# One step of a hybrid trunk layer: other buffers for cached values and sample states, other places in the engines' order

## The chip, the cores and the metric

The kernel runs on one core of a Trainium2 chip. A core has TensorE (PE: matmuls, with weight loads beside them), VectorE (DVE), ScalarE (ACT), GpSimd (POOL) and SyncE (SP, which issues transfers), each with an instruction stream of its own that runs in order, and 16 DMA engines. ACT and POOL issue transfers too. The metric is the device time of the core in microseconds, as the median of the runs; less is better.

## The reference, cut to what matters

A layer takes 1024 prompt tokens and 8 sample tokens (one new token each, with caches). The parts, in the order of the kernel:

```
p  = x @ w_in                       # 1024 -> 3592 columns: q, k, v of 8 attention heads; u (q, k, v), z, a, b of 4 delta heads
delta heads (prompt):  q, k, v = silu(causal conv(u));  q, k normalised
    chunks of tokens:  T = I + strict_lower(beta * k k^T * decay);  solve T [u | w] = [v beta | k beta e^g]
    state carried over the chunks;  o = q S;  RMS norm;  * silu(z)
delta heads (samples): S = S e^g;  mem = k S;  S = S + k ((v - mem) beta);  o = q S       # S from state_b_ssm
attention (prompt):    softmax over dilated windows (128,1) (512,4) (2048,16) with a relative bias, merged by denominators
attention (samples):   the same over cache_a_k, cache_a_v (512 rows) and the new row
h  = LayerNorm(alpha x + mix @ w_out)
y  = LayerNorm(alpha h + MoE(h))    # 4 groups x 8 experts, top 1 group, top 2 experts in it
```

Outputs: y of prompt and samples, the key and value windows, the new rows, the delta states and the convolution states. All is fp32.

## The kernel before

Products keep fp32 by a split: a number is held as a high part (a cast) and a low part (the difference), and a product is three matmuls, xh wh, xl wh, xh wl (L278 to L280, 128x344 each). `weight(c0)` loads 128 columns of w_in on SP's queue, casts the high part on ACT (`his`, L254) and subtracts the low part on DVE (`los`, L255).

The stages, by time:

- 0 to 40 us: x is loaded and transposed; the a and b columns are projected.
- 40 to 460: four delta heads. For each: features (convolution, squares for the norms with ACT L483), then the triangular solve inside 16-blocks on DVE, which is a substitution column by column (`column`, L521 to L525, then L530 to L532, columns again, and the spread of the result, L535), then the larger blocks by matmuls on PE (`inverse`), then the scan over chunks (L583 to L613) and the gate. The projections of the next columns stand between these steps in PE's order and fill its waits.
- In the same stretch, `delta_sample` (L667) does the samples' delta work: convolution on POOL, tanh on ACT (L685), products and norms; for each head it loads the 8 states (si, L673), multiplies them with k and q (pkq, 16 small matmuls, L720) and copies the result (skq, L721). A second time, after attention 0, it loads the states again, updates them on POOL (L759 to L761, with rows wb) and stores them (out_ssm_sample, L762).
- 460 to 770: attention of four pairs of heads. Each softmax step has a score matmul (L850, L851, with low key parts kl from DVE L823), a minimum on DVE (L852), exponentials on ACT (L857), transposes on PE (L866), copies pT (ACT L868, DVE L870) and the output matmul (L875). `scores_sample` loads cached keys kc and multiplies them by the query on POOL (L904), and DVE sums (L905). In the last pair w_out is loaded and split too (L1052, L1054 on ACT, L1055 on DVE).
- 750 to 950: mixing with w_out (`mixed`, L1124), the samples' attention over cached values (`attention_sample`: v loads by `cache_rows`, L773 to L779, on POOL's queue, products pav L937), the first layer norm, routing and the lists of the experts.
- 950 to 1530: 32 experts, their weights in pieces of 1 MB (`piece`, L956, on SP's queue), split on ACT and DVE (L1343, L1344).
- 1530 to 1580: the last layer norm.

Big tiles share named slots: a tile with the name of a slot waits until the last reader of the tile before it is done. The slots of 2048 columns are w (2), kq (2), dtf and xy; those of 1024 columns are U (2), acc, vt, ktl (2), vh (2), gb, ft, qk (2), zt (2), os and z2. The four cached-value tiles all lie in xy. The pieces of the first experts lie in these slots too: piece 2 and 3 in kq, 4 in dtf, 8 in xy. `PIECE_AT` says which of them are issued behind which `mixed(t)`; the others are issued before the first.

The order of each engine is fixed at compile time by a scheduler. `after(later, earlier)` (L260) adds an edge to it that has no semaphore: it only says that `later` comes behind `earlier` in the order. `SUMS` and `WOD` feed such edges: pair and softmax step behind which a sum of scores, or a w_out split, is placed.

Of the kernel before, what the change touches and what calls it, by code (L numbers as in the profile page):

```python
# [12 lines left out]
AF = mybir.ActivationFunctionType  # L13
OP = mybir.AluOpType
# [4 lines left out]
P = 128  # L19
S = 1024  # L20
NS = 8
# [3 lines left out]
NT = S // P  # L25
# [3 lines left out]
HB = 4  # L29
# [3 lines left out]
AHEAD = 2  # L33
FLY = 5
XGB, YB, WHB, AHB, EHB, ELB = 2, 1, 5, 1, 2, 2
SUMS = ((0, 8), (1, 8), (2, 4), (3, 4))
GROUPS = (4, 7, 8, 9)
RNK = ((0, 3), (4, 8), (7, 8))
PTD = 3
# [4 lines left out]
ADD = ((8, 7, 8),)  # L44
FAST = True
ATS = 3
PIECE_AT = {3: 8, 4: 6}
LATE = 29
LN_ORDER = (0, 1, 2, 3, 4, 5, 6, 7, 8)
LN_ACT = (1, 3, 5, 7, 8)  # L50
# [60 lines left out]

U_ = lambda j, h: 1536 + (4 * j + h) * P
DJ = 2
WOD = [(3, k + 1) for k in range(8)]
FIRST = (3, 6)
ABA = (1, 3)
EARLY_D = (0,)
# [5 lines left out]
def body(ctx, tc, I, O, C):  # L123
    nc = tc.nc
# [66 lines left out]
    def T8(tag, name):  # L191
        return s8.tile([P, 2048], F32, tag=tag, name=name, bufs=S8[tag])
# [22 lines left out]
    def T4(tag, name):  # L215
        n, b = W4[tag]
        turn[tag] = (turn.get(tag, -1) + 1) % b
        return four(f"{tag}{turn[tag]}", n, name)
# [24 lines left out]
    loads, his, los, decays = {}, {}, {}, {}  # L243
# [11 lines left out]
        los[c0] = nc.vector.tensor_tensor(out=lo, in0=rw, in1=hi.bitcast(F32), op=OP.subtract)  # L255
        return hi, lo

    values, parts, roots, exps, last, inverse, stores, sums, minima = {}, {}, {}, {}, {}, {}, {}, {}, {}

    def after(later, earlier):  # L260

        tc.add_manual_dep(later.ins, earlier.ins.name, mybir.DependencyInfo(mybir.DependencyClass.NoSync, mybir.DependencyReason.DATA),
                          reason="projections fill the wait for a chain")
# [38 lines left out]
    for t in range(NT + 1):  # L302
        n = P if t < NT else NS
# [4 lines left out]
        for b in range(2):  # L308
            ps = tps(f"xps{t}_{b}")
# [21 lines left out]
    for t in range(NT + 1):  # L331
        n = P if t < NT else NS
# [107 lines left out]
    def delta(h, kq):  # L440
# [34 lines left out]
        for b in range(2):  # L475
            for j, f in enumerate((q2, k2)):
                ps = tps(f"fps{h}_{b}_{j}")
                for n in range(4):
                    t = 4 * b + n
                    nc.tensor.transpose(ps[:, n, :], f[:, t * P:(t + 1) * P], ident)  # L480
                for n in range(4):
                    t = 4 * b + n
                    nc.scalar.activation(out=junk, in_=ps[:, n, :], func=AF.Square, accum_out=ss[:, j, t:t + 1])  # L483
                    if j == 1:
                        nc.vector.tensor_scalar(out=ktl[:, t, :], in0=ps[:, n, :], scalar1=etail[:, t, h:h + 1],
                                                scalar2=None, op0=OP.mult)
# [34 lines left out]
        def column(f, j0, k0, k):  # L521

            n = k - j0
            nc.vector.tensor_tensor(out=xm[:, :, :n], in0=f[:, :, :n, k - k0], in1=xb[:, :, k:k + 1].to_broadcast([P, NT, n]), op=OP.mult)
            nc.vector.tensor_tensor(out=xb[:, :, j0:k], in0=xb[:, :, j0:k], in1=xm[:, :, :n], op=OP.subtract)  # L525

        for k in range(15, 8, -1):
            column(fc, 8, 9, k)
        pr = dtf[:, S:S + 512].rearrange("p (t j k) -> p t j k", j=8, k=8)
        nc.vector.tensor_tensor(out=pr, in0=fa[:, :, :, 7:15], in1=xb[:, :, None, 8:16].to_broadcast([P, NT, 8, 8]), op=OP.mult)  # L530
        nc.vector.tensor_reduce(out=xm, in_=pr, axis=AX.X, op=OP.add)
        nc.vector.tensor_tensor(out=xb[:, :, 0:8], in0=xb[:, :, 0:8], in1=xm, op=OP.subtract)  # L532
        for k in range(7, 0, -1):
            column(fa, 0, 1, k)
        nc.vector.tensor_tensor(out=x.rearrange("p t (b j) -> p t b j", j=16), in0=xb[:, :, None, :].to_broadcast([P, NT, 8, 16]),  # L535
                                in1=m16.rearrange("p (b j) -> p b j", j=16)[:, None, :, :].to_broadcast([P, NT, 8, 16]), op=OP.mult)

        vt = yield
# [127 lines left out]
    def delta_sample():  # L666
        tps = lambda name: psd.tile([P, 4, P], F32, tag="c", name=name)  # L667
        state = I["state_b_ssm"][0].rearrange("s h d e -> d h s e")
        out = O["ssm_sample"][0].rearrange("s h d e -> d h s e")

        def state_in(h, again):
            t = T4(("ft", "z2")[h % 2] if again else "U", f"si{h}_{again}")[:, :S]
            nc.sync.dma_start(out=t.rearrange("p (s e) -> p s e", e=P), in_=state[:, h])  # L673
            return t

# [6 lines left out]
        for i in range(3):  # L682
            nc.gpsimd.tensor_tensor(out=tmp, in0=cst[:, :, i, :].rearrange("p s t -> p t s"), in1=wv(i), op=OP.mult)
            nc.gpsimd.tensor_tensor(out=acc, in0=acc, in1=tmp, op=OP.add)
        nc.scalar.activation(out=tmp, in_=acc, func=AF.Tanh, scale=0.5)  # L685
        f2 = sm_t("f2", [P, 12, NS])
        nc.vector.scalar_tensor_tensor(out=f2, in0=tmp, scalar=1.0, in1=acc, op0=OP.add, op1=OP.mult)
        q2, k2, v2 = f2[:, 0:4, :], f2[:, 4:8, :], f2[:, 8:12, :]
# [10 lines left out]
        nc.vector.reciprocal(out=pw[SH:2 * SH, 2:3], in_=pw[SH:2 * SH, 3:4])  # L699
        nc.gpsimd.tensor_tensor(out=pw[:SH, 2:3], in0=pw[:SH, 3:4], in1=nhalf[:SH, 0:1], op=OP.pow)  # L700
        roots["s"] = nc.gpsimd.tensor_tensor(out=pw[:2 * SH, 3:4], in0=pw[:2 * SH, 3:4], in1=half[:2 * SH, 0:1], op=OP.pow)
        dg = T4("os", "dg")[:3 * SH, :4 * SH]
        nc.vector.tensor_scalar(out=dg[:, :3 * SH], in0=ident[:3 * SH, :3 * SH], scalar1=pw[:3 * SH, 2:3], scalar2=None, op0=OP.mult)
        nc.vector.tensor_scalar(out=dg[:, 3 * SH:], in0=ident[:3 * SH, SH:2 * SH], scalar1=pw[:3 * SH, 3:4], scalar2=None, op0=OP.mult)
        ps = tps("spb").rearrange("p a b -> p (a b)")
# [10 lines left out]
        for h in range(HB):  # L716
            si = state_in(h, 0)
            pk = tps(f"pkq{h}").rearrange("p a b -> p (a b)")
            for s in range(NS):
                nc.tensor.matmul(pk[:, 2 * s:2 * s + 2], si[:, s * P:(s + 1) * P], f2[:, h:h + 5:4, s], start=True, stop=True)  # L720
            nc.vector.tensor_copy(out=skq[:, h], in_=pk[:, :2 * NS])  # L721

        w = sm_t("ws", [P, HB, NS])
        t1 = sm_t("t1s", [P, HB, NS])
# [9 lines left out]

        ps = tps("pwt").rearrange("p a b -> p (a b)")
        nc.tensor.transpose(ps[:SH, :P], fl(w), ident)
        wr = T4("os", "wr")[:SH, :P]
        nc.vector.tensor_copy(out=wr, in_=ps[:SH, :P])
        nc.gpsimd.dma_start(out=wr_d.rearrange("h (s e) -> (h s) e", e=P), in_=wr)
        yield  # L740
# [168 lines left out]
    def attention_sample(tps, avs):  # L909
# [15 lines left out]
        nc.vector.tensor_copy(out=p1, in_=ps[:, 0:64])  # L925
        nc.vector.tensor_copy(out=p2[:ROWS2], in_=ps[:ROWS2, 64:128])
        for pr in range(4):
            v12 = T8("xy", f"v_{pr}")
            v1, v2 = tiles(v12), tiles(v12[:, S:])
            cache_rows(v1, v2, vf, 2, pr)  # L930

            pav = tps(f"pav{pr}")
            for a in range(2):
                for n, (p_, v) in enumerate(((p1, v1), (p2, v2))):
                    r = P if n == 0 else ROWS2
                    for c in range(4):
                        nc.tensor.matmul(pav[32 * c:32 * c + 32, a, :], p_[:r, 4 * a:4 * a + 4, :].rearrange("p s h -> p (s h)"),  # L937
                                         v[:r, 4 * a + c, :], start=(n == 0), stop=(n == 1))
            av = avs[:, pr % 2 * 256:pr % 2 * 256 + 256].rearrange("p (a b) -> p a b", b=P)
            nc.scalar.copy(out=av, in_=pav[:, 0:2, :])  # L940
            pat = tps(f"pat{pr}")
            for a in range(2):
                nc.tensor.transpose(pat[:, a, :], av[:, a, :], ident)
            for j in range(2):
                r = slice(64 * j, 64 * j + 64)
                nc.vector.tensor_copy(out=mixS[r, HB + pr, :].rearrange("p (a c) -> p a c", c=4), in_=pat[r, 0:2, 2 * pr + j:2 * pr + j + 121:40])
# [122 lines left out]
        after(his[-k - 1], exps[p_][max(n - 1, 0)])  # L1069
    for h in VTD:  # L1070
        after(values[h], last[VTD[h]])
    after(roots[HB - 1], roots["s"])
    after(sums["s"], last[0, 0])
    for h in range(HB):
        if FILL[h] is not None:
# [5 lines left out]
    with ph12:  # L1081
# [214 lines left out]
            nc.vector.tensor_scalar(out=gat, in0=pl[:, NE:2 * NE], scalar1=1.0 / ALPHA, scalar2=None, op0=OP.mult)  # L1296

        for i in range(NA):
            if i not in PIECE_AT.values():
                piece(i, i)  # L1300
        for t in range(NT + 1):
            if t == ATS:
                attention_sample(tps, avs)
            if t != QS:
                mixed(t)
            else:
                mixed_samples()
            if t in PIECE_AT:
                piece(PIECE_AT[t], PIECE_AT[t])
            if t + 1 in GROUPS:  # L1310
                listed = route(max([g for g in (0,) + GROUPS if g <= t]), t + 1)
        for t, t0, i in ADD:
# [281 lines left out]
```

## Time and profile before

| what | us |
| --- | --- |
| median of 3 runs | 1577.39 |
| lowest and highest run | 1575.81, 1586.39 |
| the profiled execution | 1581.44 |
| its span, first to last instruction | 1579.7 |
| PE busy in the span | 1437.3 (91%) |
| DVE busy | 1105.5 (70%) |
| ACT busy | 879.8 (56%) |
| POOL busy | 352.4 (22%) |

The mean granted clock of TensorE is 0.94 of full speed. The rows further down come from this one execution; its times count from the first instruction. A row of a window gives its bounds, its length, the busy time (and count) of PE, of PE's weight loads, of DVE, ACT and POOL, then the granted clock as a share of full speed, the DMA share, and GB/s. In a row of instructions the bracket at the end gives the idle time of the engine just before and what ended it.

### The profile page before, as it was taken

How to read it: one execution, taken by the hardware profiler on the slowest of the kernel's cores; microseconds unless marked ns; L12 is line 12 of the kernel's file. 1: busy time of each engine (PE TensorE's matmuls, PEld its weight loads, DVE VectorE, ACT ScalarE, POOL GpSimd, SP SyncE). 2: the span in 40 equal slices, each digit the busy share in tenths (PEclk: the TensorE clock that was granted, in tenths of full speed). 3: DMA queues.
4: the chain of work that ended last, by engine and by line, in shares of the span. 5: the costliest groups of instructions: out<-in, count | busy, mean ns of one | idle time of the engine just before them, and what ended most of it. 6: DMA issues, size and time to landing. Idle time of an engine off the chain costs nothing. (4 is left out here: it accounts for less than half of the span.)

```text
span 1579.7 us, 22960 instructions
## 1 busy us (share of the span) xinstructions
PE 1437.3 (91%) x8084; PEld 1183.1 (75%) x8085; DVE 1105.5 (70%) x2105; ACT 879.8 (56%) x1754; POOL 352.4 (22%) x346
## 2 busy tenths in 40 slices
PE   5979999989999889997987988999999999999970
PEld 3969888888987768874764766888888888888860
DVE  4576686857444545355532767999999999999977
ACT  3323434432243334344320117999999999999974
POOL 7020222214022420102111112111221112211115
PEclk9989999999899989995998978999999999999995
DMA  5221110114133342325655276999999999999965
GB/s 175 101 90 41 43 41 17 53 36 113 25 110 100 128 101 67 98 97 195 180 184 129 96 280 249 359 361 373 362 355 352 361 367 365 362 353 364 341 193 215
DMA packets 140016, 309.39 MB, mean 196 GB/s; under 512 B 13483, under 2 KB 71775, under 8 KB 139888
## 3 DMA queue, kind: packets, MB, share of 16 engines
q1 hardware_dynamic: 113928, 259.21, 45.5%
q0 software_dynamic: 14720, 33.92, 8.6%
q10 hardware_dynamic: 11248, 14.75, 2.9%
q8 instruction: 65, 1.06, 0.3%
q14 instruction: 55, 0.45, 0.1%
HBM read 284.04 MB, written 45.24 MB: 208 GB/s over the span
## 5 line engine op out<-in xcount | busy, mean ns | idle before, releaser
L1344 DVE TENSOR_TENSOR wl<-p,wh 128x512 fp32r<-128x512 f32 x436 | 270.2, 685 | 1.4 <-ACT wh L1343 1.4
L1343 ACT CAST wh<-p 128x512 fp32r<-128x512 f32 x436 | 254.2, 633 | 18.8 <-PE h L1380 8.5
L278 PE MATMUL pp<-xh,w 128*128 128x344 f32 x672 | 231.8, 345 | 2.0 <-ACT w L254 1.5
L280 PE MATMUL pp<-xh,w 128*128 128x344 f32 x672 | 223.9, 333 | 9.0 <-DVE w L255 9.0
L279 PE MATMUL pp<-xl,w 128*128 128x344 f32 x672 | 224.9, 335 | 0.0
L1378 PE MATMUL h<-wh,eh 128*128 128x512 f32 x512 | 206.8, 404 | 0.0
L1379 PE MATMUL h<-wl,eh 128*128 128x512 f32 x512 | 205.6, 402 | 0.4 <-DVE wl L1344 0.4
L1380 PE MATMUL h<-wh,el 128*128 128x512 f32 x512 | 201.3, 393 | 0.0
L278 PEld LDWEIGHTS pp<-xh,w 128*128 128x128 f32 x672 | 130.6, 194 | 12.5 <-issue 6.4
L280 PEld LDWEIGHTS pp<-xh,w 128*128 128x128 f32 x672 | 130.8, 195 | 11.2 <-DVE w L255 9.3
L279 PEld LDWEIGHTS pp<-xl,w 128*128 128x128 f32 x672 | 130.8, 195 | 2.1 <-issue 1.5
L1350 POOL MEMSET xg<- 128x1024 f32 x32 | 30.5, 953 | 400.2 <-PE xp L1363 396.3
L1379 PEld LDWEIGHTS h<-wl,eh 128*128 128x128 f32 x512 | 96.7, 189 | 25.6 <-DVE wl L1344 7.9
L1344 DVE TENSOR_TENSOR wl_d<-p,wh_d 128x512 fp32r<-128x512 f32 x188 | 115.5, 684 | 0.0
L1343 ACT CAST wh_d<-p 128x512 fp32r<-128x512 f32 x188 | 109.5, 621 | 3.2
L1378 PEld LDWEIGHTS h<-wh,eh 128*128 128x128 f32 x512 | 96.9, 189 | 18.7 <-ACT eh L1365 0.2
L1380 PEld LDWEIGHTS h<-wh,el 128*128 128x128 f32 x512 | 96.5, 188 | 18.5 <-DVE el L1366 0.2
L1419 PE MATMUL py<-wh_d,al 128*128 128x512 f32 x248 | 96.9, 391 | 0.0
L1417 PE MATMUL py<-wh_d,ah 128*128 128x512 f32 x248 | 96.6, 389 | 0.0
L1418 PE MATMUL py<-wl_d,ah 128*128 128x512 f32 x248 | 96.5, 389 | 0.0
L1124 PE MATMUL op<-wo,qkm 128*128 128x512 f32 x256 | 89.7, 425 | 0.0
L857 ACT ACTIVATE sc<-sc,mx 128x128 f32<-128x128 f32 (+7 forms) x64 | 49.6, 776 | 70.7 <-DVE mx L852 63.8
(463 smaller groups left out, 2852.4 us busy)
## 6 DMA issues: line engine op xcount, KB each, us to landing
p<-in_w_up SPq DMA_DIRECT2D x58, 1024.0 KB
p<-in_w_gate SPq DMA_DIRECT2D x51, 1024.0 KB
p<-in_w_down SPq DMA_DIRECT2D x47, 1024.0 KB
rw<-in_w_in SPq DMA_DIRECT2D x28, 512.0 KB
p_vh<-in_w_down SPq DMA_DIRECT2D x12, 512.0 KB
p_ktl<-in_w_gate SPq DMA_DIRECT2D x10, 512.0 KB
p_ktl<-in_w_down SPq DMA_DIRECT2D x10, 512.0 KB
skew_d<-bias_d SPq DMA_DIRECT2D x1, 4608.0 KB
```

Of the source, the lines that this page charges most:

```text
L278: nc.tensor.matmul(ps, wh[:, k, :], xh[:, k, s], start=(k == 0), stop=False)
L279: nc.tensor.matmul(ps, wh[:, k, :], xl[:, k, s], start=False, stop=False)
L280: last[c0, g] = nc.tensor.matmul(ps, wl[:, k, :], xh[:, k, s], start=False, stop=(k == KD - 1))
L1124: mixes[t] = nc.tensor.matmul(pss[b], m[:, k, :], wo[k][:, w, cs[b]], start=(k + i == 0), stop=(k + i == KD + 1))
L1343: nc.scalar.copy(out=wh, in_=src)
L1344: nc.vector.tensor_tensor(out=wl, in0=src, in1=wh.bitcast(F32), op=OP.subtract)
L1378: nc.tensor.matmul(ps, eh[:, k, :], wh, start=(k == 0), stop=False)
L1379: nc.tensor.matmul(ps, eh[:, k, :], wl, start=False, stop=False)
L1380: nc.tensor.matmul(ps, el[:, k, :], wh, start=False, stop=(k == KD - 1))
L1417: nc.tensor.matmul(py[b], ah[:, k, :], wh, start=(k == 0), stop=False)
L1418: nc.tensor.matmul(py[b], ah[:, k, :], wl, start=False, stop=False)
L1419: nc.tensor.matmul(py[b], al[:, k, :], wh, start=False, stop=(k == 3))
```

## The change

The cached values of the four pairs get the slots dtf, kq, kq and xy. Since pieces 2, 3 and 4 use the same slots, they are now issued behind `mixed(3)`, with piece 8. The samples' states of the first pass come in halves of one kq tile and no longer in U; in the second pass in ft and os and no longer in ft and z2. Two small tiles that lay in os (dg, wr) get a tile of their own. The score sums of pairs 2 and 3 and the w_out splits move to later softmax steps. In the order, one edge goes and four come: the samples' tanh behind the last square of head 3 (ACT), the samples' state products of head 0 behind the inverse of head 3 (PE), their first copy behind the spread of head 3's substitution (DVE), and the first column of head 0's substitution behind the weight split of head 1's q columns (DVE).

```diff
-SUMS = ((0, 8), (1, 8), (2, 4), (3, 4))
+SUMS = ((0, 8), (1, 8), (2, 10), (3, 12))
...
-PIECE_AT = {3: 8, 4: 6}
+PIECE_AT = {3: (8, 4, 2, 3), 4: (6,)}
...
-WOD = [(3, k + 1) for k in range(8)]
+WOD = [(3, k + 4) for k in range(8)]
...
-                    nc.scalar.activation(out=junk, in_=ps[:, n, :], func=AF.Square, accum_out=ss[:, j, t:t + 1])
+                    squares[h] = nc.scalar.activation(out=junk, in_=ps[:, n, :], func=AF.Square, accum_out=ss[:, j, t:t + 1])
...
         for k in range(15, 8, -1):
-            column(fc, 8, 9, k)
+            i = column(fc, 8, 9, k)
+            substituted.setdefault(h, i)
...
+        si2 = T8("kq", "si2")
+
         def state_in(h, again):
-            t = T4(("ft", "z2")[h % 2] if again else "U", f"si{h}_{again}")[:, :S]
+            t = T4(("ft", "os")[h % 2], f"si{h}_{again}")[:, :S] if again else si2[:, h % 2 * S:h % 2 * S + S]
...
-        nc.scalar.activation(out=tmp, in_=acc, func=AF.Tanh, scale=0.5)
+        tanhs["s"] = nc.scalar.activation(out=tmp, in_=acc, func=AF.Tanh, scale=0.5)
...
-        dg = T4("os", "dg")[:3 * SH, :4 * SH]
+        dgw = sm_t("dgw", [P, P])
+        dg = dgw[:3 * SH, :4 * SH]
...
-                nc.tensor.matmul(pk[:, 2 * s:2 * s + 2], si[:, s * P:(s + 1) * P], f2[:, h:h + 5:4, s], start=True, stop=True)
-            nc.vector.tensor_copy(out=skq[:, h], in_=pk[:, :2 * NS])
+                i = nc.tensor.matmul(pk[:, 2 * s:2 * s + 2], si[:, s * P:(s + 1) * P], f2[:, h:h + 5:4, s], start=True, stop=True)
+                products.setdefault(h, i)
+            copies[h] = nc.vector.tensor_copy(out=skq[:, h], in_=pk[:, :2 * NS])
...
-        wr = T4("os", "wr")[:SH, :P]
+        wr = dgw[:SH, :P]
...
-            v12 = T8("xy", f"v_{pr}")
+            v12 = T8(("dtf", "kq", "kq", "xy")[pr], f"v_{pr}")
...
-    after(roots[HB - 1], roots["s"])
+    after(tanhs["s"], squares[HB - 1])
+    after(products[0], inverse[HB - 1])
+    after(copies[0], spread[HB - 1])
+    after(substituted[0], los[U_(0, 1)])
...
-            if t in PIECE_AT:
-                piece(PIECE_AT[t], PIECE_AT[t])
+            for i in PIECE_AT.get(t, ()):
+                piece(i, i)
```

## Rows read from the trace of the kernel before

**Rows 1.** Windows by stage (columns as told in the section on the profile).
```profile
0.00:960.00 960.00, 866.11 (x5415) 714.54 (x5417) 536.75 (x1173) 323.25 (x779) 216.32 (x241) 0.92 0.34 105
960.00:1530.00 570.00, 569.62 (x2665) 467.63 (x2664) 536.98 (x888) 539.04 (x950) 112.77 (x91) 1.00 0.97 351
1530.00:1579.70 49.70, 1.57 (x7) 0.96 (x6) 31.79 (x46) 17.48 (x26) 23.27 (x14) 0.56 0.53 185
```

**Rows 2.** PE's waits by releaser, whole span: total us, times, longest.
```profile
PE pav L937 <- DMA v<-in_cache_a_v: 13.5, 3, 5.3
PE pp L280 <- DVE w L255: 9.0, 1, 9.0
PE s L851 <- DVE kl L823: 6.7, 1, 6.7
...
PE o L875 <- DVE pT L870: 6.2, 3, 5.3
...
PE ks L587 <- DVE st L602: 4.4, 3, 4.0
```

**Rows 3.** Waits of SP's queue, 900 to 1530 us.
```profile
SPq L956 <- DVE wl L1344: 99.1, 50, 14.8
```

**Rows 4.** Windows behind the longest waits.
```profile
112.70:116.00 3.30, 3.25 (x11) 3.25 (x12) 0.00 (x0) 0.00 (x0) 0.14 (x1) 0.51 0.58 158
377.10:414.60 37.50, 34.27 (x186) 32.96 (x185) 15.79 (x51) 3.56 (x7) 7.00 (x8) 0.77 0.37 82
557.40:567.50 10.10, 10.10 (x32) 7.20 (x32) 3.58 (x12) 2.47 (x10) 0.56 (x1) 0.55 0.92 209
713.00:754.00 41.00, 31.80 (x101) 18.83 (x101) 23.26 (x44) 17.57 (x35) 7.68 (x5) 0.50 0.53 182
827.00:868.00 41.00, 27.49 (x190) 19.18 (x188) 8.07 (x14) 3.39 (x7) 5.87 (x9) 0.83 0.57 130
```

**Rows 5.** Timeline of DVE, 99 to 117 us: start, duration, engine, line, operation.
```profile
100.54 1.35 DVE L524 TENSOR_TENSOR xm<-xy,xb 128x56 f32<-128x56 f32 x1 [2.27 <-ACT xy L512]
...
111.48 1.22 DVE L255 TENSOR_TENSOR w<-rw,w 128x1024 fp32r<-128x1024 f32 x1
```

**Rows 6.** Timelines of ACT, and of PE, around the same wait.
```profile
101.16 1.04 ACT L254 CAST w<-rw 128x1024 fp32r<-128x1024 f32 x1
...
112.75 0.65 PE L280 MATMUL pp<-xh,w 128*128 128x344 f32 x1 [9.03 <-DVE w L255]
```

**Rows 7.** Timeline of DVE, 347 to 352 us.
```profile
349.76 0.26 DVE L687 SCALAR_TENSOR_TENSOR f<-tmps 128x96 f32<-128x96 f32 x1 [4.13 <-ACT tmps L685]
```

**Rows 8.** Timeline of PE, 384 to 402 us.
```profile
393.21 0.32 PE L278 MATMUL pp<-xh,w 128*128 128x344 f32 x1
393.37 1.84 PE L720 MATMUL pkq<-f,si 128*128 128x2 f32 x16
```

**Rows 9.** Window of head 3's substitution, matmuls of L278 alone.
```profile
377.10:414.60 37.50, 14.92 (x39) 8.79 (x39) 0.77 0.37 82
```

**Rows 10.** Timeline of DVE, 526 to 590 us.
```profile
529.80 4.71 DVE L821 TENSOR_TENSOR qs<-qT,qs 64x512 fp32r<-64x512 f32 x2 [0.19 <-ACT qs L819]
...
556.64 0.68 DVE L823 TENSOR_TENSOR kl<-kT,ksa 64x512 fp32r<-64x512 f32 x1 [10.44 <-DMA out_ssm_sample<-si]
...
583.88 1.22 DVE L905 TENSOR_REDUCE sc<-kc 128x16 f32<-128x1024 f32 x1
```

**Rows 11.** Timeline of POOL, 545 to 575 us.
```profile
553.47 0.97 POOL L777 DMA_DIRECT2D kc<-in_cache_a_k  x1 [0.30 <-POOL si L761]
...
566.94 4.71 POOL L904 TENSOR_TENSOR kc<-kc,qb 128x1024 f32<-128x1024 f32 x2 [10.62 <-DMA qb<-qkv_d]
```

**Rows 12.** Timeline of DVE, 712 to 737 us.
```profile
723.13 1.22 DVE L905 TENSOR_REDUCE sc<-kc 128x16 f32<-128x1024 f32 x1 [4.22 <-POOL kc L904]
...
727.53 0.55 DVE L870 COPY pT<-pps 128x384 f32<-128x384 f32 x1
```

**Rows 13.** Timeline of POOL, 700 to 880 us.
```profile
839.12 0.92 POOL L777 DMA_DIRECT2D v<-in_cache_a_v  x1 [12.14 <-PE pav L937]
```

More of the change, by code (lines that the diff above doesn't have):

```diff
@@ L256, in weight @@
         return hi, lo
-    values, parts, roots, exps, last, inverse, stores, sums, minima = {}, {}, {}, {}, {}, {}, {}, {}, {}
+    values, parts, roots, exps, last, inverse, stores, sums, minima, substituted, spread, squares, tanhs, products, copies = ({} for _ in range(15))
     def after(later, earlier):
@@ L523, in column @@
             n = k - j0
-            nc.vector.tensor_tensor(out=xm[:, :, :n], in0=f[:, :, :n, k - k0], in1=xb[:, :, k:k + 1].to_broadcast([P, NT, n]), op=OP.mult)
+            i = nc.vector.tensor_tensor(out=xm[:, :, :n], in0=f[:, :, :n, k - k0], in1=xb[:, :, k:k + 1].to_broadcast([P, NT, n]), op=OP.mult)
             nc.vector.tensor_tensor(out=xb[:, :, j0:k], in0=xb[:, :, j0:k], in1=xm[:, :, :n], op=OP.subtract)
+            return i
         for k in range(15, 8, -1):
-            column(fc, 8, 9, k)
+            i = column(fc, 8, 9, k)
+            substituted.setdefault(h, i)
         pr = dtf[:, S:S + 512].rearrange("p (t j k) -> p t j k", j=8, k=8)
@@ L534, in delta @@
             column(fa, 0, 1, k)
-        nc.vector.tensor_tensor(out=x.rearrange("p t (b j) -> p t b j", j=16), in0=xb[:, :, None, :].to_broadcast([P, NT, 8, 16]),
+        spread[h] = nc.vector.tensor_tensor(out=x.rearrange("p t (b j) -> p t b j", j=16), in0=xb[:, :, None, :].to_broadcast([P, NT, 8, 16]),
                                 in1=m16.rearrange("p (b j) -> p b j", j=16)[:, None, :, :].to_broadcast([P, NT, 8, 16]), op=OP.mult)
@@ L1298, in body @@
         for i in range(NA):
-            if i not in PIECE_AT.values():
+            if not any(i in at for at in PIECE_AT.values()):
                 piece(i, i)
```

## The prediction

> **What bounds the kernel.** I read the busy shares by stage first. Up to 960 us TensorE (PE) is busy 866 of 960 us at a granted clock of 0.92; from 960 to 1530, the experts, it is busy 569.6 of 570 at 1.00; behind that lies a tail of 50 us with almost no matmuls [rows 1]. So the experts run at PE's limit, and what starts them earlier ends the kernel earlier, one for one, if their weights keep up. They do: the weight queue stood 99 us in that stage waiting for buffers to come free, not for bytes [rows 3]. The question is then which of the 94 idle microseconds ahead of 960, and which of the slow-clock ones, the change takes away. PE's waits by releaser name them: 13.5 us on cached values, 9.0 on one weight split, 6.7 on attention's low keys, 5.3 on a transposed-probability copy, 4.0 on a state update [rows 2]. Last I read windows just behind these waits: the granted clock is 0.51 to 0.55 there, that is at the lower of its two levels (1.2 of 2.4 GHz), for 3.3 us after the wait that ends at 112.7 and 10 us after the one that ends at 557.4 [rows 4]. A removed wait therefore gives back its length and about half of the slow stretch behind it.
>
> **A, weight split before the substitution.** The first column of head 0's substitution starts on VectorE (DVE) at 100.54 and the low half of the next weight, L255, comes only at 111.48, behind the whole chain [rows 5]. Its cast on ScalarE (ACT) was done at 101.16 + 1.04 = 102.20 [rows 6]. The new edge puts L255 first: 102.2 + 1.22 = 103.4, and PE ran dry at 112.75 - 9.03 = 103.72 [rows 6]. The wait goes: 9.0. Behind it 3.25 us of matmuls at 0.51 become 1.6: another 1.6. The substitution ends some 2 us later; projections cover it, since PE has weights again. A = 10.6.
>
> **B, samples' delta work behind head 3.** Today ACT and DVE wait in order for the samples' tanh and product (DVE 4.13 us at L687 [rows 7]), and head 3's scan stands behind them: 4.0 on PE [rows 2]. The edge behind the last square takes that wait off: 4.0. From 377.1 to 414.6 PE then runs head 3's fill at a mean clock of 0.77, busy 34.3 us [rows 4], because sixteen-matmul groups on state tiles (pkq) and DVE copies are woven into the substitution. At full clock a projection matmul starts every 0.16 us and a pkq group takes 1.84 [rows 8]. The stretch holds 39 x 3 = 117 projection matmuls [rows 9] = 18.7 us, four pkq groups = 7.4, and 0.5 for the rest: 26.6 in place of 37.5, a gain of 10.9. The groups still run, behind inverse[3]. B = 14.9. What may come back: the states now go through two halves of one buffer, so heads 2 and 3 load only after heads 0 and 1 were read. Below, nothing (projections cover it); above, two waits like the longest one for cached values, 2 x 5.3 = 10.6 [rows 2]. I take 4, as projections are left to run.
>
> **C, second state load.** DVE stood 10.44 us at L823 until a state's output transfer had freed a slot [rows 10], and PE 6.7 behind it [rows 2]. With the states in ft and os, and no longer in z2, that slot is free: 6.7. The 10.1 us behind at 0.55 [rows 4] would take 5.6: 4.5 more. C = 11.2. What is late next: the os half waits for earlier outputs, so POOL's state products end later, and the cached keys of pair 1 are loaded right behind them, at 553.47 [rows 11]. The product of these keys starts at 566.94, its first half ends near 569.3, and the sum that reads it, on DVE in front of softmax steps, came at 583.88 [rows 10, 11]: 14.6 us of slack. Cost between 0 and a stall like the one removed, 6.7; I take 3.
>
> **D, POOL beside DVE.** DVE L821 took 4.71 us for two, beside POOL's state product, while L823 of the same size takes 0.69 [rows 10]; that is 3.3 lost once. The product moves and will meet other DVE work, so I keep 3.3 inside the last loss term below. The Trainium skill, "SBUF — State Buffer", section "Who interferes with whom", says that a DVE instruction with two inputs in SBUF contends with a GpSimd instruction that reads SBUF, and that whoever comes second is blocked for the other's whole length. The trace agrees in that one row; by the rule each later meeting costs up to one POOL product, which would add about one such loss to the sum.
>
> **E, sums and w_out splits in attention 3.** DVE waited 4.22 us at L905 for POOL's key products, and the probability copy PE waited for came only at 727.53 [rows 12]: 5.3 on PE. The sums go to steps 10 and 12 of pairs 2 and 3 and the splits three steps later, so the copy comes first: 5.3. The stretch 713 to 754 ran wholly at 0.50, with 31.8 us busy [rows 4]: full clock would give up to 15.9. The low clock began before this wait and outlasted it by 25 us, unlike A and C, so I take only 3 of that. E = 8.3. The moved splits (DVE, 1.22 for one of this size by L255 [rows 5]) fall on the end of the stage; DVE is busy 23 of its 41 us, so there is room.
>
> **F, cached values in four buffers.** Each load waits on POOL until the previous pair's product has read the one buffer (12.14 us at 839.12, on pav) [rows 13]; PE waits three times, 13.5 us together [rows 2]. With four buffers (dtf and kq come free with attention 3) no load waits for a product, and all four can be issued together ahead of the first use: 13.5. From 827 to 868 the clock averages 0.83 [rows 4], which is a third of 41 us at the lower level; 12 of these 14 us busy, halved, are 6. F = 19.5. Against it: three more expert pieces of 1 MB go behind mixed(3), with piece 8. That is 4 MB, 12 us at the experts' 351 GB/s [rows 1], in a stretch whose DMA share is 0.57 [rows 4] and that ends some 90 us before the experts. The four loads together delay weights and rows of h: between 0 and one 5.3; I take 3.
>
> **Sum.** 10.6 + 14.9 + 11.2 + 8.3 + 19.5 = 64.5. Losses: 4 (B) + 3 (C) + 3 (F), and 7 for POOL contention (3.3) and for chains of DVE and ACT that take over where PE's stall is gone. Net 64.5 - 17 = 47.5. The profiled execution took 1581.44 (span 1579.7 and 1.7 around it), 4 above the median of 1577.39: it becomes about 1534, the median 1577.4 - 47.5 = 1530.
>
> **Rivals.**
> 1. Idle goes, clock stays: the waits 9.0 + 4.0 + 6.7 + 5.3 + 13.5 = 38.5 are saved, none of the slow stretches; with the losses of 17, 21.5 are left: 1556. For it: 713 to 754 was slow with no long wait in front. Against: the clock came back within 10 us at A and C.
> 2. The clock recovers in attention 3 as well: 12.9 more, 1517. For: a 5 us hole less; against: the short holes of softmax stay.
> 3. Nothing measurable: the waits reappear under other names. Upper losses (10.6 + 6.7 + 5.3 = 22.6) with rival 1 leave 15.9, 1561.5; with one of F's or A's waits left too, 1570.
> 4. Slower, by one mechanism: POOL's second pass over the states comes so late that the sum of pair 1, standing in DVE's order in front of the softmax, holds attention 1. Slack is 14.6, then a microsecond for each. It decides only when the pass is over 80 us late (14.6 + 64.5, and 15.8 more for 1%); POOL's last state product and the key load stand at 553 [rows 11], so both would come only near 640. At 110 us late: 1577 - 50 + 95 = 1622. Against it: state loads come right behind the slots' release.
>
> **How the numbers follow.** The forecast holds 0.50 (own range 1510 to 1545), rival 1 0.22, rival 2 0.12, rival 3 0.10, rival 4 0.06. The bottom of the range is E at full clock with only 4 of the losses: 64.5 + 12.9 - 4 = 73.4, so 1504; the top is rival 1 with upper losses, 1562. One per cent (about what a measurement can tell from no change) is 15.8 us, 1561.6: faster is the forecast, rival 2 and four fifths of rival 1, 0.80; same 0.14; slower 0.06.
>
> **What would show it.** A: no wait of PE at L280 on a weight near 104. B: clock near 1.00 through head 3's substitution, pkq after it. C: L823 behind no output transfer. E: no long wait at the copy behind L905; the clock there decides between rivals 1 and 2. F: the value loads stand together on POOL and PE has no wait at pav. The stage in which PE is full starts some 47 us earlier. It is wrong if PE's idle before the experts stays above 70 us under new names, if L905 of pair 1 waits long, or if the experts wait for weight pieces.

## The result, and the profile after

The changed kernel takes 1531.18 us (median of 4 runs, 1527.0 to 1531.84), the kernel before beside it 1581.89 (median of 4, 1575.81 to 1588.86): a ratio of 0.9673, with a 95% interval of 0.9621 to 0.9724. Run twice more on other occasions it gave 0.9699 (0.9679 to 0.9720) and 0.9646 (0.9624 to 0.9668). The forecast was 1530. The ratios and intervals here and below are those of the record; they are not always the quotient of the two medians beside them.

The profiled execution took 1527.0 (span 1525.2), the one before 1581.44 (span 1579.7), so the two traces differ by 54.5 us in their spans, a few more than the medians do. The first expert's first matmul starts at 954.4 before and at 900.5 after. Windows that end and begin at these two points (bounds, length, busy time and count of PE, PE's weight loads, DVE, ACT and POOL, granted clock, DMA share, GB/s) show where the time went. Before:

```profile
0.00:954.40 954.40, 860.51 (x5397) 709.97 (x5398) 534.45 (x1169) 320.70 (x774) 214.38 (x239) 0.93 0.34 104
954.40:1579.70 625.30, 576.79 (x2688) 473.16 (x2688) 571.06 (x936) 559.07 (x980) 137.99 (x107) 0.96 0.93 336
```

After:

```profile
0.00:900.50 900.50, 838.61 (x5397) 695.12 (x5398) 530.54 (x1169) 322.00 (x774) 219.82 (x239) 0.96 0.36 110
900.50:1525.20 624.70, 576.21 (x2688) 472.97 (x2688) 570.94 (x936) 558.99 (x980) 137.60 (x107) 0.96 0.93 336
```

The work is the same: 5397 matmuls ahead of the experts in both. Experts and last norm take 625.3 and 624.7: nothing changed there. Of the 53.9 us ahead of the experts, 32.0 are idle time (93.9 before, 61.9 after) and 21.9 are busy time, that is the same matmuls at a higher granted clock (0.93 to 0.96).

PE's waits after, by releaser (total, times, longest), are to be read against [rows 2]:

```profile
PE fb L511 <- DVE dt L509: 6.3, 2, 6.1
PE pps L872 <- ACT sc L863: 6.3, 3, 4.8
PE xp L1372 <- DMA xg<-h_d,idxi: 6.1, 1, 6.1
...
PE ks L589 <- DVE so L612: 4.0, 3, 1.5
...
PE o L881 <- DVE pT L876: 0.7, 1, 0.7
PE ks L589 <- DVE st L604: 0.6, 3, 0.2
...
PE pp L280 <- DVE w L255: 0.4, 1, 0.4
```

All five waits of [rows 2] are gone or down to parts of a microsecond. Two long ones are new: 6.1 us at L511, and 4.8 at L872, where the longest was 2.1 before. The table follows the lead of the changed kernel over the one before from landmark to landmark on PE; the last column is what the prediction had for that stretch, its losses included (B and C with 4 and 3, F with 3).

| landmark on PE | before | after | lead | gained in the stretch | predicted |
| --- | --- | --- | --- | --- | --- |
| first key product of head 1 | 169.8 | 159.6 | 10.2 | 10.2 | 10.6 |
| first key product of head 3 | 342.7 | 332.4 | 10.3 | 0.1 | 0 |
| last output transpose of head 3 | 458.4 | 443.5 | 14.9 | 4.6 | 10.9 |
| last merge transposes of pair 0 | 531.1 | 516.0 | 15.1 | 0.2 | 0 |
| last merge transposes of pair 1 | 624.8 | 601.8 | 23.0 | 7.9 | 8.2 |
| last merge transposes of pair 2 | 702.2 | 679.2 | 23.0 | 0.0 | 0 |
| last merge transposes of pair 3 | 774.8 | 743.5 | 31.3 | 8.3 | 8.3 |
| first expert | 954.4 | 900.5 | 53.9 | 22.6 | 16.5 |

The landmarks of the pairs are read where the last four transposes of the row sums start. The prediction's remaining loss of 7, which it gave to no place, does not appear as such. This table rests on one execution of each kernel; the stretches in all traces stand at the end of the next section, and some of them differ from this table.

### The profile page after: what moved, and what is told of

It is laid out like the page before. It is cut to its first block, busy times and chain, and to the rows that moved or that the text cites. A ratio compares the mean times of both kernels' runs of the same rounds, so it can differ in the third digit from the quotient of the medians.

```text
span 1525.2 us, 22948 instructions
## 1 busy us (share of the span) xinstructions
PE 1414.8 (93%) x8084; PEld 1168.1 (77%) x8085; DVE 1101.5 (72%) x2105; ACT 881.0 (58%) x1754; POOL 357.4 (23%) x346
## 5 line engine op out<-in xcount | busy, mean ns | idle before, releaser
L1352 ACT CAST wh<-p 128x512 fp32r<-128x512 f32 x436 | 254.1, 633 | 18.3 <-PE h L1389 8.2
L278 PE MATMUL pp<-xh,w 128*128 128x344 f32 x672 | 227.8, 339 | 1.5 <-ACT w L254 1.5
L279 PE MATMUL pp<-xl,w 128*128 128x344 f32 x672 | 221.3, 329 | 0.0
L280 PE MATMUL pp<-xh,w 128*128 128x344 f32 x672 | 220.1, 328 | 0.4 <-DVE w L255 0.4
L278 PEld LDWEIGHTS pp<-xh,w 128*128 128x128 f32 x672 | 127.7, 190 | 11.5 <-issue 7.0
L280 PEld LDWEIGHTS pp<-xh,w 128*128 128x128 f32 x672 | 128.0, 190 | 2.3 <-issue 1.2
L1388 PEld LDWEIGHTS h<-wl,eh 128*128 128x128 f32 x512 | 96.6, 189 | 25.3 <-DVE wl L1353 7.8
L1387 PEld LDWEIGHTS h<-wh,eh 128*128 128x128 f32 x512 | 96.8, 189 | 18.6 <-ACT eh L1374 0.2
L1389 PEld LDWEIGHTS h<-wh,el 128*128 128x128 f32 x512 | 96.4, 188 | 18.6 <-DVE el L1375 0.2
L1426 PE MATMUL py<-wh_d,ah 128*128 128x512 f32 x248 | 96.6, 389 | 0.0
L1133 PE MATMUL op<-wo,qkm 128*128 128x512 f32 x256 | 84.0, 403 | 0.0
```

The lines of the kernel that those rows point to most:

```text
L278: nc.tensor.matmul(ps, wh[:, k, :], xh[:, k, s], start=(k == 0), stop=False)
L279: nc.tensor.matmul(ps, wh[:, k, :], xl[:, k, s], start=False, stop=False)
L280: last[c0, g] = nc.tensor.matmul(ps, wl[:, k, :], xh[:, k, s], start=False, stop=(k == KD - 1))
L1133: mixes[t] = nc.tensor.matmul(pss[b], m[:, k, :], wo[k][:, w, cs[b]], start=(k + i == 0), stop=(k + i == KD + 1))
L1352: nc.scalar.copy(out=wh, in_=src)
L1387: nc.tensor.matmul(ps, eh[:, k, :], wh, start=(k == 0), stop=False)
```

## The experiments

The first four kernels are the one before with one part of the change each, the last of them with two. Three dots in a diff stand for lines left out: names that the edges need, the small tile of the samples, a loop over the pieces.

**A alone.**

```diff
...
     after(roots[HB - 1], roots["s"])
+    after(substituted[0], los[U_(0, 1)])
```

> The kernel before with one new edge: the first column of head 0's substitution behind the weight split of head 1's q. Theory (by the prediction): 9.0 us of PE's wait go and 1.6 of the slow stretch behind it, 10.6 faster. In the trace of the changed kernel the first inverse stands 10.3 earlier (131.7 against 142.0). Rival (the gain needs the other parts, since a later chain takes the time back): under 4 us faster.

Measured: 1569.6 beside 1581.13, a ratio of 0.9895 (0.9849 to 0.9940): 11.5 us between the medians, 16.6 by the ratio, with 9.5 to 23.9 in its interval. The wait of 9.0 is gone from its trace and the first inverse of head 0 starts at 131.8, as in the changed kernel (131.7). A stands by itself.

**E alone.**

```diff
-SUMS = ((0, 8), (1, 8), (2, 4), (3, 4))
+SUMS = ((0, 8), (1, 8), (2, 10), (3, 12))
...
-WOD = [(3, k + 1) for k in range(8)]
+WOD = [(3, k + 4) for k in range(8)]
```

> The kernel before with the sums of pairs 2 and 3 and the w_out splits at their later steps, nothing else. Theory: 5.3 of the wait for the copy and 3 of the slow stretch, 8.3 faster; in the changed kernel attention 3 took 64.3 in place of 72.6, 8.3 less. Rival 1 (idle alone, clock stays): 5.3. Rival 2 (clock recovers wholly): 21.

Measured: 1574.98 beside 1581.13, 0.9944 (0.9914 to 0.9973): 6.2 us. By the ratio it is 8.9, with 4.3 to 13.6 in the interval. That is far from rival 2's 21; it does not tell rival 1's figure (idle alone, 5.3) from the theory's 8.3.

**F alone.**

```diff
-PIECE_AT = {3: 8, 4: 6}
+PIECE_AT = {3: (8, 4, 2, 3), 4: (6,)}
...
-            v12 = T8("xy", f"v_{pr}")
+            v12 = T8(("dtf", "kq", "kq", "xy")[pr], f"v_{pr}")
...
```

> The kernel before with the cached values in four buffers and the three pieces behind mixed(3), nothing else. Theory: 13.5 of waits and 6 of slow clock less 3 for crowding, 16.5 faster. In the changed kernel the stretch from the end of attention to the first expert took 157.0 in place of 179.6, so by the trace 22.6 faster. Rival (transfers wait on POOL behind something else, or crowd out the pieces): 8 or less.

Measured: 1563.33 beside 1581.13, 0.9866 (0.9826 to 0.9905): 17.8 us, 21.2 by the ratio (15.0 to 27.5). The theory's 16.5 lies within that, and so does the 22.6 of the trace. PE has no wait at pav any more.

**B and C alone**: the samples' delta work as in the change (states, small tile, three edges on the samples, one edge removed), all else as before.

```diff
...
-            t = T4(("ft", "z2")[h % 2] if again else "U", f"si{h}_{again}")[:, :S]
+            t = T4(("ft", "os")[h % 2], f"si{h}_{again}")[:, :S] if again else si2[:, h % 2 * S:h % 2 * S + S]
...
-    after(roots[HB - 1], roots["s"])
+    after(tanhs["s"], squares[HB - 1])
+    after(products[0], inverse[HB - 1])
+    after(copies[0], spread[HB - 1])
```

> The kernel before with all of the samples' delta work as changed (states in kq halves, then ft and os, own tile for the diagonals, three edges on the samples, one edge removed), nothing else. Theory by the prediction: 14.9 + 11.2 less 7 = 19 faster. By the traces of the whole change, in which the heads after the first gave 4.6 and attention 0 and 1 gave 8.1: 12 to 13 faster, since a wait for the samples' roots (6.1 on PE) and one of ACT for a state's store (4.8 on PE) are new.

Measured: 1566.22 beside 1581.13, 0.9884 (0.9845 to 0.9923): 14.9 us, 18.3 by the ratio (12.2 to 24.5), which leaves both the prediction's 19 and the 12 to 13 read from the traces. PE's waits of this kernel show the new one of head 3, without any of the other parts, while the longest one at L872 is 2.1, as in the kernel before:

```profile
PE fb L511 <- DVE dt L509: 6.3, 2, 6.1
...
PE pps L872 <- ACT sc L863: 4.5, 4, 2.1
```

By the medians the four parts give 11.5 + 6.2 + 17.8 + 14.9 = 50.4 together, the whole change 50.7; by the ratios they give 65 and 52, with intervals of 9 to 14 us on each. The kernel before ran between 1574.70 and 1590.14 beside these four, so the times alone do not show well that the parts add; the stretches at the end of this section show it better.

The next kernels start from the changed one. It was run again beside them.

> The changed kernel again, beside the next three on one chip: 50 us faster than before, as in its first runs.

Measured: 1530.75 beside 1578.23, 47.5 faster.

**The samples' diagonal products out of the way.** The timeline of DVE in the changed kernel, 348 to 372 us (start, duration, engine, line, operation, idle before and its releaser), names what stands in front of head 3's second L509:

```profile
361.10 0.66 DVE L509 TENSOR_TENSOR dt<-fdg,cd 128x480 f32<-128x480 f32 x1
366.43 1.94 DVE L708 TENSOR_SCALAR dgw<-cm,pws 96x96 f32<-96x96 f32 x1 [4.67 <-POOL pws L704]
368.25 0.64 DVE L509 TENSOR_TENSOR dt<-fdg,cd 128x480 f32<-128x480 f32 x1
369.34 0.24 DVE L709 TENSOR_SCALAR dgw<-cm,pws 96x32 f32<-96x32 f32 x1 [0.45 <-POOL pws L705]
```

L708 waits for the samples' root on POOL, and POOL's timeline shows that root behind head 3's own work:

```profile
363.97 1.89 POOL L548 TENSOR_TENSOR vh<-vh,nk 128x1024 f32<-128x1024 f32 x1
365.82 0.57 POOL L704 TENSOR_TENSOR pws<-pws,nhalf 32x1 f32<-32x1 f32 x1
```

The first try puts L708 and L709 behind the spread:

```diff
...
+    after(copies["dg"], spread[HB - 1])
+    after(copies["nk"], spread[HB - 1])
     after(tanhs["s"], squares[HB - 1])
```

> The changed kernel with two more edges: the samples' two diagonal products on VectorE (L708, L709) behind the spread of head 3's substitution. Theory: VectorE stood 4.7 us at L708 for the samples' root on POOL, with head 3's L509 behind it, and PE 6.1 behind that with a clock of 0.75 in that window; this wait is the part of B that did not come, so the kernel is 6 to 9 us faster than the changed one. Rival 1 (POOL's own work for head 3 is late as well, so the wait moves to the matmuls behind it): 2 or less. Rival 2 (the four groups of state products cost what is missing in B, the root does not): 2 or less, with no wait at L511.

Measured: 1528.05 beside 1578.23, 0.9694 (0.9665 to 0.9723), against 1530.75 and 0.9699 of the changed kernel: 2.7 us less by the medians, no gain that can be told. The expectation missed, and the waits of PE from 355 to 400 us say how:

```profile
PE spb L711 <- DVE dgw L709: 5.0, 1, 5.0
PE fb L511 <- DVE dt L509: 0.3, 1, 0.3
```

The wait at L511 went as foretold, and one of nearly the same length came at L711, the matmul that reads the diagonals: its place in PE's order had stayed where it was, while the diagonals now came later.

**The same, with the matmul that reads them moved as well**, beside the changed kernel on another chip:

```diff
...
+    after(sums["s"], inverse[HB - 1])
     after(copies["dg"], spread[HB - 1])
     after(copies["nk"], spread[HB - 1])
```

> The kernel with the diagonal products behind the spread, and the matmul that reads them (L711) placed behind the inverse of head 3 as well. In the first try that matmul stood in PE's order before the products were there and waited 4.95 us, which gave back most of the gain. Theory (the root of the samples is what B lost): no wait at L511 and none at L711, 6 to 9 us faster than the changed kernel. Rival (the fill of head 3 is short of work, so a wait appears at the inverse): 3 or less, with PE waiting for the spread of the substitution or for the products of states.

> The changed kernel beside the next three on one chip: 48 to 50 us faster than before.

Measured: 1523.11 beside 1585.35, 0.9605 (0.9577 to 0.9633); the changed kernel 1529.14, 0.9646 (0.9624 to 0.9668). That is 6.0 us less than the changed kernel by the medians, the lower end of what was expected, though the two intervals still overlap a little. Its waits of PE from 355 to 400 us hold nothing long:

```profile
PE ops L632 <- POOL os L614: 0.7, 1, 0.7
PE fb L511 <- DVE dt L509: 0.3, 1, 0.3
```

and head 3's substitution runs full. The window 360 to 400 of the changed kernel, and of this one:

```profile
360.00:400.00 40.00, 33.67 (x192) 31.05 (x193) 17.94 (x53) 7.98 (x14) 11.99 (x11) 0.83 0.30 77
```
```profile
360.00:400.00 40.00, 39.73 (x269) 37.74 (x268) 25.36 (x74) 9.76 (x20) 12.18 (x12) 0.96 0.37 93
```

In the same 40 us PE does 269 matmuls in place of 192. From head 3's first key product to its last output transpose this kernel takes 101.5 us (334.4 to 435.9), the changed one beside it 111.0 (331.1 to 442.1). The stretch is 9.5 shorter. The spans, 1521.3 and 1527.4, differ by 6.1 only, mostly because this execution was 3.2 later already at the first key product of head 0 (81.0 against 77.8), ahead of anything that the edit touches. Windows of the whole stretch, of the kernel before, the changed one and this one:

```profile
342.70:458.40 115.70, 106.57 (x661) 95.81 (x660) 60.95 (x149) 40.36 (x122) 29.66 (x38) 0.91 0.23 61
```
```profile
332.40:443.50 111.10, 101.21 (x662) 91.18 (x661) 62.18 (x149) 40.91 (x122) 32.72 (x38) 0.94 0.24 68
```
```profile
334.40:435.90 101.50, 97.54 (x659) 88.49 (x657) 64.37 (x149) 40.94 (x122) 32.24 (x38) 0.98 0.27 74
```

With the wait gone the stretch gains 14.2 on the kernel before, where step B had 14.9 ahead of its losses.

**The states in xy.** The other new wait, at L872, goes back to ACT in the changed kernel, which stood at L889 for a state's store, in front of the exponentials:

```profile
ACT moa L889 <- DMA out_ssm_sample<-si: 6.2, 1, 6.2
```

The tile it writes lies in os, and so does a state since the change. The experiment moves the second pass to xy:

```diff
-            t = T4(("ft", "os")[h % 2], f"si{h}_{again}")[:, :S] if again else si2[:, h % 2 * S:h % 2 * S + S]
+            if again and h % 2 == 0:
+                turn["sx"] = T8("xy", f"sx{h}")
+            t = (turn["sx"] if again else si2)[:, h % 2 * S:h % 2 * S + S]
```

> The changed kernel with the states of the second pass in halves of xy, which is free at that time, in place of ft and os. Theory: ACT stood 6.2 us in attention 1 for the store of a state in os, in front of the exponentials, and PE 4.8 behind it with a slow stretch after it; without that 5 to 9 us faster than the changed kernel. Rival (sum of the key products, L905, late because the states' pass holds POOL, takes its place): 2 or less, with a long wait of VectorE at the sums of pair 1.

Measured: 1545.54 beside 1578.23, 0.9785 (0.9762 to 0.9809): 14.8 us slower than the changed kernel. The expectation was wrong because its premise was: xy is not free at that time, since attention's split queries (qs, in `stacked`) lie in it. ACT's waits from 500 to 560 us:

```profile
ACT qs L827 <- DMA out_ssm_sample<-sx: 18.6, 1, 18.6
```

The wait at the merge tile did go, but the queries of pair 1 now wait for both states' stores, and PE stood 11.0 us at its first score matmul. The run says nothing on the price of the wait at L889; it shows that a slot's tenants over the whole stage have to be listed before a tile is moved to it.

**Both at once.**

> Both of these on the changed kernel. If the two waits are independent, the two gains add, 11 to 18 us faster than the changed kernel; if the second takes over what the first gives, less than the sum.

Measured: 1541.63, 0.9759 (0.9737 to 0.9781): the loss by xy with, by the medians, 3.9 less than in x_si. Since the first edit has its own new wait and the second a false premise, this decides nothing on whether the two gains add.

**The states in ft and z2 again**, C's slots undone in the changed kernel:

```diff
-            t = T4(("ft", "os")[h % 2], f"si{h}_{again}")[:, :S] if again else si2[:, h % 2 * S:h % 2 * S + S]
+            t = T4(("ft", "z2")[h % 2], f"si{h}_{again}")[:, :S] if again else si2[:, h % 2 * S:h % 2 * S + S]
```

> The changed kernel with the states of the second pass in ft and z2 again, as before the change. Theory: the wait of L823 (now L829) for a state's store comes back, 6 to 11 us with its slow stretch, and the wait of ACT at L889 for os goes, so 4 to 8 us slower than the changed kernel. Rival (the edges on the samples moved this work so early or late that the slot no longer matters): within 2 of it.

Measured: 1534.28 beside 1585.35, 0.9677 (0.9648 to 0.9707), the changed kernel 0.9646 (0.9624 to 0.9668): 5.1 us slower by the medians, with intervals that overlap. PE's waits have the old one back, longer than in [rows 2], and the one at L872 is no longer among the long ones:

```profile
PE s L857 <- DVE kl L829: 9.0, 1, 9.0
```

So os is the better slot by the medians; the stretches below show the same, 91.3 against 84.7 to 85.8 for this stage.

**The cached values in one buffer again**, with the pieces left at their new place:

```diff
-            v12 = T8(("dtf", "kq", "kq", "xy")[pr], f"v_{pr}")
+            v12 = T8("xy", f"v_{pr}")
```

> The changed kernel with all cached values in xy again, the three pieces left behind mixed(3). Theory: the three waits at pav come back with the slow stretches, so 17 to 22 us slower than the changed kernel. Rival (part of F's gain is the later place of the pieces, not the buffers): 10 slower or less.

Measured: 1546.94 beside 1585.35, 0.9753 (0.9730 to 0.9776): 17.8 us slower than the changed kernel by the medians, the same size as F alone. The three waits are back:

```profile
PE pav L943 <- DMA v<-in_cache_a_v: 13.8, 3, 5.4
```

F's gain is the buffers'; the later place of the pieces costs and brings nothing that shows here.

**The stretches in all traces.** Each of these kernels left a trace, and in most of them a given stretch runs the same code. So a stretch can be compared over many executions, without the part of the change that acts on it and with it (lengths in us; x_si, x_both and x_z2 are left out in the third row and x_dg, x_dg2 and x_both in the second, as their edits act there):

| stretch on PE, start to start | part | without it | with it | gain by the middle values | predicted |
| --- | --- | --- | --- | --- | --- |
| first key product of head 0 to that of head 1 | A | 91.2, 91.4, 91.4, 91.7 | 80.5 to 80.6 (10 traces) | 10.8 | 10.6 |
| first key product of head 3 to its last output transpose | B | 115.8, 115.9, 116.1, 116.1 | 110.9 to 111.6 (7) | 4.8 | 10.9 |
| last merge transposes of pair 0 to those of pair 1 | C | 93.7, 96.4, 96.6, 96.8 | 84.7 to 85.8 (7) | 11.3 | 8.2 |
| those of pair 2 to those of pair 3 | E | 67.1, 70.0, 72.7, 72.7 | 62.7 to 66.1 (10) | 6.7 | 8.3 |
| those of pair 3 to the first expert | F | 174.7, 175.6, 175.8, 178.0, 179.5 | 156.7 to 159.8 (9) | 17.4 | 16.5 |

The gains sum to 51.0, the size of the whole change, and the stretches between these five stay the same within a microsecond: the parts add. The kernel before, in the one execution that the prediction and the first table read, was the shortest of its four in the third row, and the longest or level with the longest in the last two.

## Why the prediction was right, and where not

**The size and the mechanism.** The time came out near where the sum put it, 50.7 gained against 47.5, and mainly for its reasons: the five waits of [rows 2] went, with slow stretches behind them, and the experts began 53.9 us earlier in the traces (the prediction said some 47). The split into idle and clock was also about right: 38.5 of waits were counted, and most of the other 26 (64.5 less 38.5) as slow clock; 32.0 and 21.9 came, each net of what was lost. That the time itself fell within 1.2 us of the forecast is in part luck. The 47.5 were taken from a median of 1577.39; from the 1581.89 measured beside the changed kernel they would have given 1534.4. And errors of several microseconds cancelled: by the stretches in all traces B brought 6 less than its net and C 3 more, and the five together fell 3.5 short of their 54.5, where the sum had kept 7 for no place.

**A.** Predicted 10.6; 10.2 at the landmark, 10.8 by the stretch in all traces, 11.5 alone by the medians. Right, both terms.

**B's gain was sized right and its loss was not, and this is the step that failed.** The prediction had 14.9 less 4; head 3's stretch gave 4.6, and 4.8 in all traces. So some 10 were lost in place of 4, and at another place. The prediction costed the added edges by what they take out of the substitution, and priced what stands behind them only for the reload of states. The samples' chain is not only pkq: tanh, norms, roots and diagonals come later too when tanh stands behind head 3's last square, and they then meet head 3's own roots on POOL and its L509 on DVE. The prediction asked what would wait behind the reload, and not what would wait on the engines that the rest of the chain passes through. The wait is shown by p_BC, where it appears without the other parts, and its price by x_dg2: there it is gone, and 9.5 us of the stretch and 6.0 of the time with it, so that 14.2 of the 14.9 stand in the trace. The reload of states, for which 4 were set aside, shows no wait of PE. The clock also fell behind the state products, which the sum had at full clock (last section); since it does so in x_dg2 too, with under 2 us lost there against some 3 (estimates from the windows of 2 us), it can be no large part of the 9.5 between the two kernels. One reading was wrong without changing the sum: the 4.0 at L587 was the scan of head 2, still running between head 3's first products, and not head 3's.

```profile
351.62 0.77 PE L587 MATMUL ks<-st,kq 128*128 128x128 f32 x2 [3.96 <-DVE st L602]
```

**C was under-sized: its gain came and its loss did not show.** Predicted 8.2; 7.9 at the landmark against the one execution of before, 11.3 by all traces, which is the 11.2 of the sum without the loss of 3. L829 waits for no store any more. The loss was put on the sums of pair 1, which waited 2.1 us on DVE:

```profile
560.59 1.22 DVE L911 TENSOR_REDUCE sc<-kc 128x16 f32<-128x1024 f32 x1 [2.14 <-POOL kc L910]
```

What the prediction had not looked at is ACT's wait at the merge tile in os: it asked who waits for z2 and not who waits for os. ACT waits there for a state's store in every trace with states in os, 6.2 us in the profiled run of the changed kernel and 2.8 to 3.6 in the six others, and PE's longest wait at L872 is 4.8 there and 1.3 to 2.2 in the others. But the stage took hardly longer for it. Before, in the changed kernel, and in its next run:

```profile
531.10:624.80 93.70, 84.60 (x513) 67.51 (x512) 44.52 (x96) 31.46 (x66) 25.70 (x19) 0.89 0.38 105
```
```profile
516.00:601.80 85.80, 81.01 (x513) 64.69 (x511) 39.71 (x93) 32.01 (x66) 27.69 (x19) 0.96 0.45 120
```
```profile
517.00:602.30 85.30, 81.01 (x513) 64.51 (x512) 39.19 (x93) 31.89 (x66) 27.61 (x19) 0.96 0.43 121
```

So the long wait cost about a microsecond. What the shorter one costs that all of them share is not shown, since x_si, which was to remove it, failed for another reason.

**E was right at the landmark by luck, and by other terms.** 8.3 were predicted and came between the two first traces. Alone it gave 6.2 by the medians, and 6.7 by the stretch in all traces, where the kernel before varies most (67.1 to 72.7). The stretch from pair 2's last transposes to pair 3's, before and after:

```profile
702.20:774.80 72.60, 62.02 (x302) 40.73 (x301) 39.96 (x85) 29.72 (x58) 14.07 (x14) 0.72 0.50 166
```
```profile
679.20:743.50 64.30, 60.64 (x300) 39.90 (x298) 40.71 (x85) 29.70 (x58) 17.45 (x15) 0.76 0.59 179
```

Idle time fell from 10.6 to 3.7, by 6.9, and busy time by only 1.4 where 3 were counted. Even that 1.4 is not shown to be a gain of the change: p_A, whose attention 3 has the old order, had less busy time and a higher clock there.

```profile
695.00:762.10 67.10, 57.26 (x303) 37.91 (x302) 39.77 (x85) 29.62 (x58) 14.14 (x14) 0.80 0.54 180
```

Rival 2, that the clock recovers in attention 3, is out: it stays low there with hardly any wait left (0.62 from 690 to 730 us, PE busy 36.7 of 40), as the caution in step E had it.

**F was right.** Predicted 16.5; 17.8 alone and 17.8 by undoing the buffers, by the medians, and 17.4 by all traces. The 22.6 at the landmark is too much, as the kernel before had its longest such stretch in that execution. The windows from pair 3's last transposes to the first expert, before and after:

```profile
774.80:954.40 179.60, 150.94 (x893) 112.25 (x892) 91.61 (x254) 26.62 (x61) 28.46 (x38) 0.88 0.57 180
```
```profile
743.50:900.50 157.00, 141.59 (x896) 107.31 (x895) 91.12 (x254) 26.78 (x61) 25.44 (x34) 0.94 0.61 212
```

The idle time fell by 13.3 (28.7 to 15.4), as predicted (13.5). The busy time fell by 9.3 here, where 6 were counted. No loss of 3 for crowded transfers shows by itself; in all traces it would be hidden in the spread.

**D.** POOL's state products do still meet DVE's work with two inputs: a weight split of 1.2 us took 2.04 in attention 1 of the changed kernel, at 543.42, beside POOL's products of 542.46 to 547.7:

```profile
543.42 2.04 DVE L255 TENSOR_TENSOR w<-rw,w 128x1024 fp32r<-128x1024 f32 x1
```

One such meeting of 0.8 us is small against the 3.3 that were kept for it, and it is not new: before, the same line took 2.66 at 541.49. The long one of [rows 10], 4.71 for two at L821, is gone (1.41 for the two) and comes back when the states lie in z2 again, as x_z2's timeline of DVE shows, beside POOL's products of 516.10 to 520.79:

```profile
516.68 4.66 DVE L827 TENSOR_TENSOR qs<-qT,qs 64x512 fp32r<-64x512 f32 x2 [0.19 <-ACT qs L825]
```

The Trainium skill ("SBUF — State Buffer", "Who interferes with whom") says that a DVE instruction with two inputs in SBUF contends with a GpSimd instruction that reads SBUF. Both rows agree with it: they take 2.04 and 4.66 us beside POOL's products, and 1.22 and 1.41 without. How often this happens follows from where the states' pass falls.

**Rivals.** Rival 1, no gain by the clock, is refuted by the 21.9 us of busy time. Rival 3, waits under new names, held for one place that cost some 10 us (L511), and for a second (L872) that cost little, not for all. Rival 4 did not come: pair 1's sum waited 2.1 us, far from the 80 at which it would have decided.

**A faster version.** x_dg2, the changed kernel with the samples' diagonals behind head 3's spread and the matmul that reads them behind its inverse, has the lowest median of all that ran, 1523.11.

## What to carry to other kernels

When work is moved later with an order edge, list every instruction of its chain on every engine and ask for each what stands behind it in its new place; here the costly one was a small product on VectorE that waited for GpSimd, six instructions down the chain from the edge. The wait that was removed by moving its waiting instruction reappeared at the next reader until that reader was moved too (x_dg against x_dg2). Before a tile moves to another slot, write down all tenants of that slot over the stage: one forgotten tenant cost 14.8 us of the kernel with xy, and with os it made ScalarE wait 2.8 to 6.2 us. Read a stretch in several executions before a gain is put down to it: here the same code took 67.1 to 72.7 us in one stretch and 174.7 to 179.5 in another.

## What the runs showed of the hardware

The granted clock fell without idle time close in front of it. In the changed kernel TensorE is busy without a gap from 370 us on, and so in each of these windows of 2 us; first come projections and one transpose of the inverse, then from 390.06 on the state products, 32 matmuls with two columns each in 4.74 us. In their course the clock goes to its lower level, for about 6 us, and the rest of the inverse runs at that level:

```profile
388.00:390.00 2.00, 2.00 (x15) 1.98 (x14) 0.00 (x0) 0.00 (x0) 0.00 (x0) 1.00 0.22 65
390.00:392.00 2.00, 2.00 (x21) 2.00 (x19) 0.06 (x1) 1.06 (x2) 0.00 (x0) 1.00 0.04 8
392.00:394.00 2.00, 2.00 (x13) 2.00 (x13) 0.11 (x1) 0.00 (x0) 0.00 (x0) 0.59 0.28 69
394.00:396.00 2.00, 2.00 (x11) 2.00 (x12) 0.59 (x2) 0.43 (x1) 0.00 (x0) 0.50 0.68 207
396.00:398.00 2.00, 2.00 (x10) 2.00 (x9) 0.00 (x0) 0.74 (x2) 0.00 (x0) 0.50 0.79 229
398.00:400.00 2.00, 2.00 (x15) 2.00 (x15) 0.69 (x1) 0.00 (x0) 0.00 (x0) 0.71 0.08 24
```

So the clock fell there without a wait: six microseconds at about half speed, some 3 us lost (an estimate from these windows). In x_dg2 it did the same behind the first two groups of state products (from 384.4), with 0.72 and 0.50 from 388 to 392 and TensorE busy throughout. The other two groups of the changed kernel, at 400.07 and 403.42 between matmuls of the inverse, were followed by no fall: 1.00 from 400 to 420. Which of the operations in front of the fall matters, no run separated, and it stays open.
